# Closing a hand-written section ahead of the last store of a batched matrix product

One Trainium2 chip, one core. The metric is the device time of one execution in microseconds (us), lower is better. A store has *landed* when the last of the 16 DMA engines that share it has counted up its semaphore.

## The reference

```python
x: [16, 768, 512] f32      y: [16, 768, 1024] f32
out = np.einsum('bkm,bkn->bmn', x, y).astype(np.float32)      # [16, 512, 1024]
```

75.5 MB are read and 33.6 MB written. The kernel casts to bf16 on the chip, multiplies on TensorE and writes f32.

## The kernel before

The whole kernel body is one section of hand-written synchronisation (`tile_critical`) inside a Tile context. Tile is the layer that orders instructions and places semaphores by itself; in the section it leaves that to the author. SyncE issues all loads and stores; store `b` follows four steps behind its loads; VectorE casts, TensorE multiplies, ScalarE copies PSUM (the memory that TensorE writes its sums to) to one of five output buffers. At the end SyncE waits until every store has landed, then the section closes, then the context.

```python
    LAG = 4
    NO = 5
    ctx.enter_context(tc.tile_critical())          # closes when the function returns
    ...                                            # buffers, semaphores, loads' helper (cut)
    def store(b):
        if b < B - 2:
            nc.sync.wait_ge(groups, 2 * (b + 2))
        else:
            nc.sync.wait_ge(outs, b - (B - 3))
        nc.sync.dma_start(o_v[b], ob[b % NO][:]).then_inc(so[b % NO], 16)

    for b in range(B):
        ...                                        # loads of x and y (cut)
        if b >= LAG:
            store(b - LAG)
    for b in range(B - LAG, B):
        store(b)
    ...                                            # VectorE, GpSimd, TensorE (cut)
    for b in range(B):                             # ScalarE
        if b >= NO:
            nc.scalar.wait_ge(so[b % NO], 16 * (b // NO))
        for g in range(2):
            nc.scalar.wait_ge(groups, 2 * b + g + 1)
            cp = nc.scalar.copy(...)               # ob <- ps, half of the output of b
            if b < B - 1:
                cp.then_inc(room, 1)
        if b == B - 2:
            nc.scalar.drain().then_inc(outs, 1)
    cp.then_inc(outs, 1)

    for i in range(NO):
        nc.sync.wait_ge(so[i], 16 * len(range(i, B, NO)))
```

## Time and profile before

| of the kernel before | |
|---|---|
| timed | 262.55 us median of 3 (262.53 to 262.94) |
| the profiled execution | 261.94 us, span 260.2 us |
| last copy of ScalarE ends | 251.19 us |
| last store issued, landed | 251.22, 258.93 us |
| landing to end of span | 1.23 us |

The span runs from the first to the last instruction of the program in one profiled execution; times inside it count from its start.

### The profile page before, as it was taken

Reading aid. Unit: us, or ns where it says so; the run is one execution under the profiler, and the core shown is the slowest. Engines: PE = TensorE matmul, PEld = TensorE weight load, DVE = VectorE, ACT = ScalarE, POOL = GpSimd, SP = SyncE. Lnnn points to the kernel's source line nnn. Section 1 sums busy time; section 2 is a strip of 40 time slices with the busy share of each in tenths; the row PEclk is TensorE's granted clock in tenths of the full one; section 3 lists DMA queues with packets and bytes.
Section 4 is the critical chain, followed back from the end, with each engine's and each line's share of the span. In section 5 each row is a group of like instructions: output and inputs, shape, how many; then the busy total and the mean of one; then the engine's idle time right before and its main releaser. Section 6 shows DMA issues by size and latency. Waiting matters only on the chain. (4 is left out here: it accounts for less than half of the span.)

```text
span 260.2 us, 2506 instructions
## 1 busy us (share of the span) xinstructions
PE 188.3 (72%) x768; PEld 90.3 (35%) x768; DVE 82.0 (32%) x33; ACT 61.1 (23%) x33; POOL 0.2 (0%) x4
## 2 busy tenths in 40 slices
PE   0019999998938959499491995949869697785930
PEld 0004555554513525244250352514424243442410
DVE  0261644525241152511425214252232523125000
ACT  1000442243220222203222022220412204031220
POOL 0000000000000000000000000000000000000000
PEclk9999999999995979979999597997968989997985
DMA  7999989999999999999999999999999999999995
GB/s 272 418 476 408 476 378 469 393 368 461 438 398 469 388 479 423 411 441 393 458 431 441 433 388 464 408 436 446 396 456 418 464 416 423 451 385 431 438 403 227
DMA packets 4514, 109.07 MB, mean 419 GB/s; under 512 B 768, under 2 KB 768, under 8 KB 768
## 3 DMA queue, kind: packets, MB, share of 16 engines
q1 hardware_dynamic: 4512, 109.05, 98.3%
q14 instruction: 2, 0.02, 0.0%
HBM read 75.50 MB, written 33.55 MB: 419 GB/s over the span
## 5 line engine op out<-in xcount | busy, mean ns | idle before, releaser
L149 PE MATMUL ps<-yb,xb 128*128 x768 | 188.3, 411 | 61.0 <-PEq L144 61.0
L149 PEld LDWEIGHTS ps<-yb,xb 128*128 x768 | 90.3, 118 | 158.5 <-issue 92.6
L165 ACT COPY ob<-ps 128x2048 f32<-128x2048 f32 x32 | 59.8, 1869 | 184.8 <-PE ps L149 184.8
L127 DVE CAST yb<-ys 128x6144 bf16<-128x6144 f32 (+1 forms) x17 | 53.8, 3171 | 86.5 <-DMA ys<-in_y_dram 86.5
L123 DVE CAST xb<-xs 128x3072 bf16<-128x3072 f32 x16 | 28.2, 1760 | 69.7 <-DMA xs<-in_x_dram 65.2
L165 ACT ACT_TABLE_LOAD x1 | 1.3, 1283 | 5.3 <-issue 5.3
L189 POOL MEMSET const-bfloat16-1.0<- 128x1 bf16 x1 | 0.1, 102 | 0.0
L189 POOL MEMSET const-uint8-127<- 128x1 uint8 x1 | 0.1, 102 | 0.0
L189 POOL MEMSET const-float32-1.0<- 128x1 f32 x1 | 0.1, 99 | 0.0
L189 POOL MEMSET const-float32-0.0<- 128x1 f32 x1 | 0.1, 98 | 0.2 <-issue 0.2
## 6 DMA issues: line engine op xcount, KB each, us to landing
ys<-in_y_dram SPq DMA_DIRECT2D x16, 3072.0 KB, 28.2
out_dram<-ob SPq DMA_DIRECT2D x16, 2048.0 KB, 32.6
xs<-in_x_dram SPq DMA_DIRECT2D x16, 1536.0 KB, 29.8
```

The costliest lines, as they stand in the source:

```text
L123: nc.vector.tensor_copy(xb[:, i], xs[i][:]).then_inc(cast, 1)
L127: nc.vector.tensor_copy(yb[:, i, ks], ys[i][:, ks]).then_inc(cast, 1)
L149: mm = nc.tensor.matmul(ps[g][:, m, nt], x_w[:, bass.ds(s, 1), kt, mo], yb[:, bass.ds(s, 1), kt, nt * NF:(nt + 1) * NF], start=(kt == 0), ...
L165: cp = nc.scalar.copy(ob[b % NO][:, g * HB:(g + 1) * HB].rearrange("p m (t f) -> p m t f", f=NF), ps[g][:])
L189: nc = _bacc.Bacc("TRN2", target_bir_lowering=False, num_devices=1)
```

## The change

The intent is to take the closing of the section off the end of the kernel: the section closes while the queue is still busy with earlier stores; the last store is issued behind it by Tile, which also waits for it as it leaves the context. The hand-written waits shrink to stores 11, 12 and 13.

```diff
-    ctx.enter_context(tc.tile_critical())
+    section = ExitStack()
+    section.enter_context(tc.tile_critical())
...
-    for b in range(B - LAG, B):
+    for b in range(B - LAG, B - 1):
         store(b)
...
-    for i in range(NO):
-        nc.sync.wait_ge(so[i], 16 * len(range(i, B, NO)))
+    for b in range(B - LAG - 1, B - 2):
+        nc.sync.wait_ge(so[b % NO], 16 * (b // NO + 1))
+    section.close()
+
+    nc.sync.dma_start(o_v[B - 1], ob[(B - 1) % NO][:])
```

## The prediction

> **What bounds the kernel now.** I read the page of the kernel before first: the slices and the chain that ended last. Then I asked for four stretches of time around the last store, and last for SyncE's own waits and for every instruction of three source lines: the final waits (L174), the section's opening line, to which its closing code is also booked (L45), and the context's exit (L200).
>
> ```profile
> PE 188.3 (72%) x768; PEld 90.3 (35%) x768; DVE 82.0 (32%) x33; ACT 61.1 (23%) x33; POOL 0.2 (0%) x4
> ...
> DMA  7999989999999999999999999999999999999995
> ...
> PE 5%; ACT 1%; issue 0%
> ...
> out_dram<-ob SPq DMA_DIRECT2D x16, 2048.0 KB, 32.6
> ```
>
> The DMA row has 9 in nearly every slice, right up to the second last; no compute engine is above 72%. The chain explains only 6% of the span, because it starts at the last copy of ScalarE (end 251.2 us) and cannot go back through a DMA queue. So the bound is the transfers: 109 MB. A store takes a median of 32.6 us from issue to landing, because it queues behind loads and stores. From 41 to 251 us the queue moved 428 GB/s at a share of 1.00. Nothing in the change touches that body; whatever happens, happens after about 249 us.
>
> The end is read from two views. First the stretches (the last two columns are the share of the 16 DMA engines and GB/s; each stretch is 0.61 us, about one 16 KB packet on one engine, so share times 16 is the number of engines that began a packet in it):
>
> ```profile
> 251.40:252.01 0.61, 0.00 (x0) 0.00 (x0) 0.00 (x0) 0.00 (x0) 0.00 (x0) 0.63 0.44 188
> 252.01:252.62 0.61, 0.00 (x0) 0.00 (x0) 0.00 (x0) 0.00 (x0) 0.00 (x0) 0.50 1.01 430
> ...
> 256.20:256.81 0.61, 0.00 (x0) 0.00 (x0) 0.00 (x0) 0.00 (x0) 0.00 (x0) 0.50 1.01 430
> 256.80:257.41 0.61, 0.00 (x0) 0.00 (x0) 0.00 (x0) 0.00 (x0) 0.00 (x0) 0.50 0.26 108
> 257.41:258.02 0.61, 0.00 (x0) 0.00 (x0) 0.00 (x0) 0.00 (x0) 0.00 (x0) 0.50 0.19 81
> ```
>
> At 251.4 only 7 of 16 engines have work: the others are done with the second last store and starve until the last one, issued at 251.22, arrives at 252.05. After 256.8 only 4 engines, then 3, are moving data. These late ones never starved: their last packets start at 257.94 in the trace's packet records, and 8 packets of 0.611 us each make the store's share of an engine, so the latest began its share at 257.94 - 7 x 0.611 = 253.67, straight after its share of the store before. Those few set the landing at 258.93.
>
> Second, what SyncE does after that landing (SPq and the like are the sequencers; durations in ns, then first and last start in us):
>
> ```profile
> L45 SPq EVENT_SEMAPHORE  x3: 17/28/28, 259.1 to 259.3; - x3
> L45 SPq NOP  x2: 13/13/13, 0.7 to 259.4; - x2
> L45 SPq COMPARE_BRANCH  x1: 33/33/33, 258.9 to 258.9; - x1
> ...
> L174 SPq EVENT_SEMAPHORE  x2: 27/28/28, 251.6 to 254.1; - x2
> L200 SPq DRAIN  x3: 7/7/7, 259.4 to 259.8; - x3
> SPq L45 <- DMA out_dram<-ob: 4.8, 1, 4.8
> SPq L174 <- DMA out_dram<-ob: 2.5, 1, 2.5
> ```
>
> The five final waits have been folded into two semaphore instructions and into the section's closing branch: the branch at 258.944 carried the last of them (4.8 us of waiting). From there the section closes (one increment by SyncE, a DRAIN on each engine, two waits and a NOP on SyncE), which ends at 259.41. The context's exit follows, beginning with SyncE's DRAIN at 259.445 and ending with the span at 260.16. So there are two joins in a row after the last byte: 259.445 - 258.944 = 0.50 us for the section, 260.16 - 259.445 = 0.715 us for the context.
>
> **What the Trainium skill says.** "DMA: Bandwidth & Descriptors", Specifications, gives a fabric ceiling of 435 GB/s; the 428 GB/s of the long stretch agrees that the body is at the transfers' limit (and lies above the 358 GB/s that the same table gives as HBM's share of a core, so the measurement decides there). The same page, Queues, rings and completion order, says that each DMA engine consumes a queue's descriptors in ring order and that a semaphore increment lands only after that engine's earlier writes. The trace agrees: the stores' landings are 4.86, 4.87, 4.80 us apart at the end (244.40, 249.27, 254.13 and 258.93 for the last four). So the last store's full count of 16 also covers the second last store, for which the new code no longer waits. The same page, Latency and other measured facts, puts the first byte at about 600 ns; here it is 0.83 us from the issue, and I use that. "VectorE: DVE Perf Modes", The DRAIN you can't avoid, separates constant boilerplate DRAINs of about 12 ns from pipeline flushes; those at the end here are 7 to 64 ns, so what a join costs is the semaphore steps between engines.
>
> **The change, part by part.**
>
> (1) Removed: the five final waits. They take no time of their own; they end when the data land. Gain 0.
>
> (2) Added: three waits, for stores 11, 12 and 13. They landed at about 239.6, 244.4 and 249.27, all ahead of the end of ScalarE's last copy at 251.19. Cost 0, off the path.
>
> (3) Moved: the section's close, from after the landing to before the last issue. Its branch and SyncE's increment can now run at about 249.3, while ScalarE still copies. What is left after the copy: ScalarE's DRAIN and increment (before, the DRAIN of an earlier copy cost about 0.035 us more than the plain increment), one semaphore wait on SyncE and the NOP, 0.06 us each by their spacing at 259.27, 259.33, 259.40 and 259.445. That is 0.15 to 0.2 us, against 0.026 us from copy to issue now. So the last store is issued at about 251.35 to 251.45 in place of 251.22, 0.15 to 0.2 us later.
>
> (4) What the later issue costs. It moves the first packets of the starving engines from 252.05 to about 252.25. Those engines are done at 257.13, and the latest one at 258.56: they have 1.4 us to spare. The late engines need the descriptors by 253.67, 1.6 us after 252.05. Cost 0, as the delay is below 1.4 us.
>
> (5) The tail. The landing stays at 258.93; now the context's exit waits for it, at its first DRAIN or just ahead, and then takes its 0.715 us. The section's 0.50 us are gone from after the landing. Gain 0.50 us, less some 0.06 us if the exit gets a wait instruction of its own.
>
> Sum: span 260.2 - 0.5 = 259.7 us. The timed median lies 2.35 us above the profiled span (262.55 against 260.2) through what comes ahead of and after it; none of that changes. 262.55 - 0.45 = 262.1 us, 0.2% less.
>
> **Rivals.**
>
> A. The later issue reaches the end: the close costs more on SyncE than I think, and engines starve for it. Against it: 1.4 us to spare. If the close took all its 0.50 us after the copy, the landing would still not move. Only a delay over 1.4 us would eat into the gain, and one of 1.9 us would cancel it: 262.5.
>
> B. The last store is made to wait for the second last one too, through a dependence that Tile sees on the output or through a full join of queues. The issue would then be at about 254.3, and all engines would starve. From an issue to the first engines' count took 257.325 - 251.218 = 6.1 us, so the landing would be near 260.4, 1.5 us later than now, and the sum 262.55 + 1.5 - 0.5 = 263.5 us. For it: hand-written waits leave out exactly that store, and I have not seen what Tile makes of it. Against it: the section's raw semaphores are unknown to Tile, which can only wait for the section as a whole.
>
> C. The join is not removed but taken over: the exit now has waits of its own for a DMA and every engine, so that only 0.1 to 0.2 us go away: 262.4. The exit's DRAINs and semaphores (L200) exist before already and would only get one more wait, so I give this less weight.
>
> D. The body shifts by a changed instruction layout or another alignment of loads: no view shows a stall of that kind, and with DMA at 1.00 it would not show anyway.
>
> **Range and chances.** The mechanism makes 262.0 to 262.1; C and partial A 262.3 to 262.5; B 263.5. Three runs of before spread over 0.41 us, almost as much as the effect. I take 262.1, with 261.6 to 262.7 for 8 in 10. A 2% change would need 5.25 us, ten times the whole section's close, and nothing that follows the last landing is that long (1.23 us in all): faster 0.01, same 0.97, slower 0.02.
>
> **What would show it.** In the profile after: the last store issued at 251.3 to 251.5, counted from the span's start, with three stores waited for before 249.5; the section's DRAINs and semaphores (L45) between 249 and 251.5 and none after the landing; the last landing within 0.2 us of 258.9; from landing to the span's end 0.7 to 0.8 us in place of 1.23; the span near 259.7; 4 or 3 engines still at work at the end. I am wrong if the last store is issued after 252.5 (A) or after 254 (B), if more than 1 us follows the landing (C), or if the median moves by more than 0.7 us either way.

## The result, and the profile after

| | before | after |
|---|---|---|
| timed, first set | 262.54 us (4 runs, 262.36 to 262.94) | 262.27 us (4 runs, 261.99 to 262.47) |
| ratio of that set | | 0.9987, 95% interval 0.9970 to 1.0004 |
| profiled execution: last copy ends | 251.19 | 250.66 |
| last store issued | 251.22 | 250.88 |
| second last store landed | 254.13 | 255.09 |
| last store landed | 258.93 | 259.90 |
| landing to end of span | 1.23 | 0.79 |

A ratio is the mean time of one kernel's fast runs over that of the other's of the same rounds, so it is not quite the ratio of the medians quoted beside it. The change is within 2%, and slightly on the fast side. One set does not exclude zero; the experiments add two more.

The page of the changed kernel, the same rows as before:

```profile
span 260.7 us, 2506 instructions
...
PE 186.1 (71%) x768; PEld 89.8 (34%) x768; DVE 82.0 (31%) x33; ACT 61.1 (23%) x33; POOL 0.2 (0%) x4
...
DMA  7998999999899899989999989999998999999994
...
PE 9%; ACT 1%; issue 0%
```

The body is the same: DMA at 9 or close to it throughout, compute engines below 72%. Yet the profiled span is longer than before (260.7 against 260.2), although less happens after the landing. The profiled execution took 262.47 us, the slowest of its four; the one of before, 261.94, was faster than any of the four that were timed in that set. Two single executions cannot be subtracted here. They can be compared part by part.

First SyncE's instructions, by source line, in the changed kernel (durations ns min/median/max, then first and last start in us). L46 is the section, L175 the three waits, of which one has been folded into the section's branch, L181 the store that Tile issues, L207 the context's exit; the lines are picked from the views of these four and from that of the waits:

```profile
L175 SPq EVENT_SEMAPHORE  x1: 28/28/28, 250.2 to 250.2; - x1
L46 SPq COMPARE_BRANCH  x1: 33/33/33, 250.3 to 250.3; - x1
L46 SPq EVENT_SEMAPHORE  x3: 17/28/28, 250.5 to 250.7; - x3
L46 ACTq DRAIN  x1: 171/171/171, 250.5 to 250.5; - x1
L46 SPq NOP  x1: 13/13/13, 250.8 to 250.8; - x1
L181 SPq DMA_DIRECT2D out_dram<-ob x1: 332/332/332, 250.9 to 250.9; - x1
L207 SPq EVENT_SEMAPHORE  x3: 17/17/17, 259.9 to 260.6; - x3
L207 SPq DRAIN  x3: 7/7/7, 260.0 to 260.3; - x3
SPq L207 <- DMA out_dram<-ob: 8.7, 1, 8.7
```

The whole close, which before stood at 258.9 to 259.4 behind the landing, now stands at 250.3 to 250.8. ScalarE's DRAIN (171 ns here, 14 ns in e2, where the last copy was over before it) waits for the last copy, and the store follows 0.22 us after that copy instead of 0.03. The wait of 8.7 us for the last store has moved from the section's branch to the exit, where one wait (259.916 in the trace) stands ahead of the DRAIN (259.970): 0.05 us of new cost. From landing to end it is 0.79 us.

Then the DMA engines near the end of the changed kernel, as in the prediction (the last two columns are their share and GB/s):

```profile
251.40:252.01 0.61, 0.00 (x0) 0.00 (x0) 0.00 (x0) 0.00 (x0) 0.00 (x0) 0.68 1.02 430
...
256.20:256.81 0.61, 0.00 (x0) 0.00 (x0) 0.00 (x0) 0.00 (x0) 0.00 (x0) 0.50 0.32 134
256.80:257.41 0.61, 0.00 (x0) 0.00 (x0) 0.00 (x0) 0.00 (x0) 0.00 (x0) 0.50 0.25 107
257.41:258.02 0.61, 0.00 (x0) 0.00 (x0) 0.00 (x0) 0.00 (x0) 0.00 (x0) 0.50 0.13 54
258.02:258.63 0.61, 0.00 (x0) 0.00 (x0) 0.00 (x0) 0.00 (x0) 0.00 (x0) 0.50 0.06 27
258.63:259.24 0.61, 0.00 (x0) 0.00 (x0) 0.00 (x0) 0.00 (x0) 0.00 (x0) 0.50 0.06 27
```

All 16 engines begin a packet between 251.4 and 252.0, where 7 did before, because the copy happened to end earlier. Some ran dry here too, but sooner: by the packet records 8 of 16 had one in flight at 251.7, just when the first packets of the last store began. Most are done by 256.8; two go on (0.13 of 16), then a single one (0.06 of 16) to 259.5. So here the last landing is set by one engine that was late. The lateness was there before the change could act: store 13 had landed at 250.23, against 249.27 in the profile of before, and the section's branch comes only at 250.32. The second last store lands at 255.09, against 254.13, and the last one 4.81 us after that one here, 4.79 us there.

### The profile page after: what moved, and what is told of

It is laid out like the page before. It is cut to its first block, busy times and chain, and to the rows that moved or that the text cites. A ratio compares the mean times of both kernels' runs of the same rounds, so it can differ in the third digit from the quotient of the medians.

```text
span 260.7 us, 2506 instructions
## 1 busy us (share of the span) xinstructions
PE 186.1 (71%) x768; PEld 89.8 (34%) x768; DVE 82.0 (31%) x33; ACT 61.1 (23%) x33; POOL 0.2 (0%) x4
## 5 line engine op out<-in xcount | busy, mean ns | idle before, releaser
L150 PE MATMUL ps<-yb,xb 128*128 x768 | 186.1, 407 | 62.7 <-PEq L145 60.7
```

The source lines that it names most:

```text
L150: mm = nc.tensor.matmul(ps[g][:, m, nt], x_w[:, bass.ds(s, 1), kt, mo], yb[:, bass.ds(s, 1), kt, nt * NF:(nt + 1) * NF], start=(kt == 0), ...
```

## The experiments

My theory, in three parts: (a) closing the section costs about 0.5 us of SyncE's time wherever it stands, and behind the landing this is paid in full; (b) the later issue is free, because the latest DMA engines set the end and still have earlier work; (c) the landing's own scatter has nothing to do with the change. The main rivals: the landing comes later by as much as the tail got shorter; Tile's issue, not the early close, is what helps; the running dry of some engines matters.

**The changed kernel again, twice (e1, e9).** Edit: none.

> The changed kernel again, with more rounds, to size the gain. My theory (the section's 0.50 us leave the tail, 0.06 us of a new wait come in, the landing doesn't move): 0.4 to 0.5 us faster than before, ratio 0.9981 to 0.9985. Rival D0 (the landing moves later by about as much as the tail got shorter, as the one profile pair would have it: last landing 259.9 against 258.9): no gain, ratio 0.9995 to 1.001. In its profile both agree on 0.7 to 0.8 us from landing to the end.

> The changed kernel once more, to size the gain with the last set (two sets gave 0.9987 with intervals of 0.0016 either way). My theory: 0.44 us less after the landing (1.23 to 0.79 us in the profiles), the landing unchanged on average: ratio 0.9979 to 0.9989. Rival (the landing gives it back): 0.9995 or above.

Measured: e1 261.81 us (6 runs) against 262.51 (11 runs), ratio 0.9987 (0.9971 to 1.0003); e9 261.91 us (6) against 262.22 (11), ratio 0.9985 (0.9962 to 1.0007). With the first set these are three sets that agree; weighted by their intervals and taken as independent they give 0.9987, give or take 0.0010, so 0.35 us less (0.0013 x 262.5). That excludes no gain, if barely, and includes the 0.44 us of the tail; taken by itself no set does exclude it. The rival's range (0.9995 and above) is touched only at the upper end. e1 lies just outside the range expected of it, e9 inside. In all three profiles of the changed kernel 0.79 us follow the landing, and the last store lands 4.81, 4.84 and 4.82 us after the second last.

**One part alone: close early, issue by hand (e2, e10).**

```diff
-    for b in range(B - LAG, B - 1):
+    for b in range(B - LAG, B):
...
-    nc.sync.dma_start(o_v[B - 1], ob[(B - 1) % NO][:])
+    with tc.tile_critical():
+        nc.sync.wait_ge(so[(B - 1) % NO], 16 * ((B - 1) // NO + 1))
```

(With the wait written bare, in no section, the program did not build: its scheduling reported a deadlock. So it has no run.)

> One part alone: the last store is still issued by hand, inside the section (so 0.03 us after the copy, not 0.2), the five-engine section closes while it flies, and a second section holding only SyncE's wait for it stands behind. My theory: the close of five engines is off the tail, a close of one engine remains, 0.1 to 0.3 us; so 0.2 to 0.4 us faster than before, between before and the change. Rival (what helps is Tile's own issue of the store): no faster than before, ratio 0.9995 to 1.0005.

> The kernel with the second, SyncE-only section once more (0.9996 in the first set, its profile had 1.12 us after the landing against 1.23 before and 0.79 in the change): ratio 0.9990 to 1.0001, slower than the changed kernel of the same rounds by 0.2 to 0.4 us.

Measured: 262.29 us, 0.9996 (0.9983 to 1.0009), and 262.14 us, 0.9996 (0.9973 to 1.0019): 0.1 us, less than the 0.2 to 0.4 expected at first, and inside the range that the first expectation gave to its rival (0.9995 to 1.0005); e10 came out as expected, 0.3 us slower than the changed kernel of its rounds by the ratios (0.9996 - 0.9985). The times alone cannot tell why, the trace can. The lines of e2 after the landing, SyncE only, picked from two views (L208 is the exit, L181 the second section):

```profile
L208 SPq COMPARE_BRANCH  x1: 33/33/33, 259.4 to 259.4; - x1
L181 SPq EVENT_SEMAPHORE  x1: 17/17/17, 259.6 to 259.6; - x1
L181 SPq DRAIN  x1: 7/7/7, 259.7 to 259.7; - x1
L181 SPq NOP  x1: 13/13/13, 259.7 to 259.7; - x1
L208 SPq DRAIN  x3: 7/7/7, 259.8 to 260.1; - x3
```

A section of SyncE alone costs almost as much to close as one of five engines. From the branch at 259.413 to the exit's DRAIN at 259.775 it is 0.36 us, and a folded wait lies ahead of the branch; 1.14 us follow the landing, in both profiles (the 1.12 in the second expectation was a misreading), against 1.23 before and 0.79 in the change. The largest step is the branch itself, 0.155 us to the next instruction. So what is costly is SyncE's own series of branch, increment, DRAIN and NOP, and less the join of the other engines: of the 0.50 us before, two waits for other engines (0.06 and 0.07 us) are what drops out. My picture of a "join" was off here. It also says which half of the change matters: the wait for the last store must be in no section of its own, otherwise most of the cost is back behind the landing. In the change it is Tile's; issue and wait by Tile were not tried apart from each other, as the bare wait did not build.

**A later issue (e3, e11, e4).** In the changed kernel, ahead of the close, with n = 8 and n = 80:

```diff
+    nc.sync.wait_ge(outs, 2)
+    for _ in range(n):
+        nc.sync.sem_inc(idle, 1)
     section.close()
```

> The changed kernel with SyncE made to wait for ScalarE's last copy ahead of the close and then to do 8 semaphore steps of 0.067 us: the last store is issued about 1.0 us later than in the change (0.54 for the steps, 0.45 for the close, which now all lies after the copy). My theory (1.4 us to spare at least, because the latest DMA engines set the end): same time as the changed kernel within 0.15 us, and the same 0.7 to 0.8 us after the landing. Rival A (a later issue reaches the end): 1.0 us slower than the change.

> The changed kernel with the issue 0.7 to 1.0 us later once more (0.9992 in the first set): my theory says as the changed kernel of the same rounds within 0.2 us; the rival that a later issue reaches the end, 0.7 us or more slower than that.

> The same with 80 steps: issue 5.9 us later than in the change. My theory: 5.9 us less what there is to spare, 1.4 (profile of before) to 2.7 us (profile of after): 3.2 to 4.5 us slower than the change, about 265.4 to 266.8. Rival A (no slack): 5.9 us slower, 268.1. All 16 engines should begin and end the last store almost together.

Measured for n = 8: 262.02 us, 0.9992 (0.9979 to 1.0005), and 262.20 us, 1.0001 (0.9979 to 1.0022). The issue is 0.96 us after the copy in both profiles, 0.74 us later than in the change, and still the last store lands 4.82 us after the second last and 0.80 us remain. So these two executions lost nothing by it. The timed medians are 0.21 and 0.29 us above the change's of the same rounds, a little more than I allowed and well below the 0.7 to 1.0 of the rival. By the means of these runs e3 is 0.07 us slower and e11 0.44 us (95% intervals of 0.5 and 0.3 us either way), so the second is clear of zero. Part of that cannot come from the landing: the timed result exceeds the span by 1.92 us in the profiled executions of e2, e3, e10 and e11, and by 1.77 to 1.78 in the nine others, before and change among them; no view here shows why. Less this 0.14 us, e3 is 0.07 us faster and e11 0.30 us slower. So the full cost of the delay is excluded, a part of it is not: whether some executions with less lag pay for the delay stays open.

Measured for n = 80: 265.42 us, ratio 1.0124 (1.0097 to 1.0152), so 1.37% or 3.6 us above the change (1.0124 - 0.9987), while the issue came 5.5 us later (5.71 us after the copy against 0.22). About 1.9 us were absorbed, 0.7 us either way (its four runs lie between 264.42 and 266.29); in the profiled execution 2.7 us: the store landed at 262.22, which is 2.8 us later than 4.82 us after the second last (254.59). The stretches of that kernel show what absorbing means:

```profile
254.00:255.00 1.00, 0.00 (x0) 0.00 (x0) 0.00 (x0) 0.00 (x0) 0.00 (x0) 0.50 0.00 0
255.20:256.60 1.40, 0.00 (x0) 0.00 (x0) 0.00 (x0) 0.00 (x0) 0.00 (x0) 0.50 0.00 0
256.60:257.21 0.61, 0.00 (x0) 0.00 (x0) 0.00 (x0) 0.00 (x0) 0.00 (x0) 0.50 1.01 430
```

Once the queue has run empty, all 16 engines start together, and the 16 landings lie within 0.20 us of each other, in place of 1.5 to 2.9 us in the change. The lag of the late engines is what pays for a late issue. Both the time and the even start are as expected.

**Ten sections more behind the landing (e5).** Stores and waits in the section as before, then:

```diff
+    section.close()                               # the section's opening is as in the change (cut)
+    for _ in range(10):
+        with tc.tile_critical():
+            for e in (nc.tensor, nc.vector, nc.scalar, nc.gpsimd, nc.sync):
+                e.nop()
```

> All stores and waits in the section as before, and ten sections more behind it, each with one NOP on each of the five engines: ten joins more after the last landing. My theory (a section's join after the last landing is paid one to one in the timed median, 0.50 us for a close, something more for an opening): 5 to 7 us slower than before. Rival C (joins overlap or hide in what comes after the kernel): under 2 us.

Measured: 270.80 us against 262.39, ratio 1.0311 (1.0294 to 1.0329), so 8.2 us slower, above my 5 to 7. The trace says the same: 9.38 us follow the landing in place of 1.23, 8.15 more.

```profile
L182 SPq EVENT_SEMAPHORE  x30: 17/28/28, 260.9 to 268.4; - x30
L182 SPq NOP  x20: 13/13/18, 260.5 to 268.5; - x20
```

A section with nothing in it but a NOP on each engine (the trace has no record of these) takes 0.82 us on average. Nine of the ten steps from one to the next are 0.76 to 0.78 us, one is 1.19 and unexplained. The first took 0.77 (from its NOP at 260.521 to the next one's at 261.287), 0.25 of it for opening (to the branch at 260.770), the rest for the close and the step to the next. I had reckoned too little for the opening. What matters for (a): time behind the landing goes one to one into the timed result (8.2 for 8.15). So the 0.44 us of the change's tail are real time, too small for three sets of runs to size well.

**The wait for the second last store put back (e6).**

```diff
-    for b in range(B - LAG - 1, B - 2):
+    for b in range(B - LAG - 1, B - 1):
```

> The changed kernel with the hand-written wait for the second last store put back, so the section can close only when it has landed (rival B of the prediction made real). My theory: issue 0.6 us after that landing, then 6.1 to 6.9 us to the next landing in place of 4.8; so 1.5 to 2.5 us slower than the change. A theory in which the queue needn't be fed ahead of time: no slower than the change.

Measured: 264.26 us, ratio 1.0072 (1.0057 to 1.0088), so 1.9 us slower than before and 2.2 (1.0072 - 0.9987) than the change, as expected. The last store is issued at 255.02, 0.63 us after the landing it waited for, and lands at 261.34. This is the prediction's rival B made real; it costs more than the 1.0 us written there, which left the close out of the way to the issue (254.3 supposed, 255.0 found).

```profile
253.60:254.40 0.80, 0.00 (x0) 0.00 (x0) 0.00 (x0) 0.00 (x0) 0.00 (x0) 0.50 0.00 0
254.40:255.80 1.40, 0.00 (x0) 0.00 (x0) 0.00 (x0) 0.00 (x0) 0.00 (x0) 0.50 0.00 0
255.85:256.46 0.61, 0.00 (x0) 0.00 (x0) 0.00 (x0) 0.00 (x0) 0.00 (x0) 0.50 1.01 430
```

No packet starts for over 2 us, then all engines start one. The change is right to leave this store out of its waits.

**The last store in halves (e7 on the kernel before, e8 on the change).**

```diff
+        nc.sync.dma_start(o_v[b, :, :HB], ob[b % NO][:, :HB]).then_inc(so[b % NO], 16)   # b = 15: after its first copy
+        nc.sync.wait_ge(outs, 3)
+        nc.sync.dma_start(o_v[b, :, HB:], ob[b % NO][:, HB:]).then_inc(so[b % NO], 16)   # e7; in e8 without then_inc, by Tile, behind the close
+    ...                                            # ScalarE's count after the first copy; e7's last wait counts both halves (cut)
```

> The kernel before with its last store cut in two, the first half issued after the first of the two last copies (5 us earlier), so that no DMA engine runs dry at 251 to 252 us. My theory (the few latest engines set the end, and they never ran dry): same as before within 0.2 us. Rival (the starving of 9 of 16 engines for up to 0.8 us sets the end): 0.4 to 0.8 us faster.

> The two together: first half by hand in the section, the second half issued behind it by Tile. My theory: as the changed kernel within 0.2 us. Rival: 0.4 to 0.8 us faster than the changed kernel.

Measured: e7 262.60 us, ratio 1.0012 (0.9998 to 1.0026); e8 262.43 us, ratio 1.0000 (0.9986 to 1.0014). Neither is faster. In e7 the engines no longer run dry (a share of 0.98 at 251.4 where before had 0.44):

```profile
251.40:252.01 0.61, 0.00 (x0) 0.00 (x0) 0.00 (x0) 0.00 (x0) 0.00 (x0) 1.00 0.98 416
...
258.02:258.63 0.61, 0.00 (x0) 0.00 (x0) 0.00 (x0) 0.00 (x0) 0.00 (x0) 0.50 0.13 54
```

and still two engines are at work at 258.02, and the landing comes 4.84 us after the second last store's. So the running dry of the early engines did not set the end. e8 has the change's 0.79 us tail, but came out about 0.3 us above the change's ratio, more than the 0.2 us expected, and e7 0.3 us above before; the intervals overlap, and whether halves cost something by themselves is open. The two differ by 0.3 us in the same rounds (1.0012 - 1.0000), the change's gain once more, though not clear of noise.

No version beat the changed kernel beyond noise.

## Why the prediction was right

- **The bound, and where the change acts**: right. The body moves the same 428 to 429 GB/s from 41 to 251 us in both kernels.
- **(1), (2) waits removed and added cost nothing**: right, though closer than said. Store 13 landed at 250.23 in the profiled execution, 0.43 us ahead of the copy's end, not 2 us (the test "before 249.5" failed with it); SyncE's part of the close and the copy ended almost together. In e1 it was 1.9 us ahead.
- **(3) the issue is 0.15 to 0.2 us later**: 0.22, 0.19 and 0.22 us after the copy in three profiles, against 0.03. Right; the absolute 251.35 to 251.45 was not (250.88), as the copies end anywhere from 249.7 to 251.6 us.
- **(4) the later issue costs 0, with at least 1.4 us to spare**: supported for the most part. 0.74 us more left no mark in two traces, though a part of it may show in the times of e11; of 5.5 us more some 1.9 were absorbed on average. One reading under it was wrong: "at 251.4 only 7 of 16 engines have work" takes the packets begun in a stretch for the engines at work at its start. By the packet records 12 were at work at 251.4 and 7 at 252.0; the engines run dry one after the other. The sum rests on the last packets and is not touched.
- **(5) 0.50 us leave the tail, 0.06 come back**: 1.23 to 0.79 us, so 0.44. Right to the step: 0.05 us for the new wait.
- **The landing stays at 258.93, within 0.2 us**: this test failed as I wrote it (259.90). In eleven profiles of kernels that issue within 1 us of the copy or in halves, changed or not, the last landing lies between 258.93 and 259.98, always 4.79 to 4.85 us after the second last store's, which itself lies between 254.13 and 255.13. The scatter is that of the late engines, there already before the change acts: the second last landing lies between 254.13 and 255.13 in three profiles with the body of before (before, e5, e7) and between 254.17 and 255.09 in the other eight. The span of 259.7 failed with it: 260.7, 260.1 and 260.1 in three profiles.
- **The 2.35 us between timed median and span**: mis-sized, as I set a span against the median of other, slower executions. Of one execution it is 1.78 us in both profiles (262.47 - 260.69, 261.94 - 260.16). As only a difference was taken, no harm came of it.
- **The sum, 0.45 us less**: 0.27 us by the medians of the first set, 0.35 us by the ratios of three. The median predicted was 262.1; 262.27, 261.81 and 261.91 were found. That the medians fit proves little: the range of 261.6 to 262.7 also holds the median of before, 262.54, so no gain at all would have passed. The mechanism rests on the 0.44 us of the tail, the same in three profiles, and on e5.

Rival A is refuted as a full cost of small delays, B did not happen (and costs 1.9 us when made to), C is refuted by the 0.79 us. For D, a body moved by the change, there is no sign in the landings above.

## What to carry to other kernels

Work behind the last landing is paid one to one, so look in the profile at what SyncE does after it, instruction by instruction, and move what does not depend on the data ahead of the last issue, as long as the queue still has earlier work to cover the delay. Do not wait for that earlier work, or the cover is gone. Size such a change by the part of the trace it touches and not by subtracting two spans: here single executions of one kernel scatter by up to 1.7 us (261.22 to 262.94 for before), the gain is 0.4.

## What the Trainium skill lacked or had wrong

- "DMA: Bandwidth & Descriptors", Latency and other measured facts, gives about 600 ns to the first byte and does not say from where it counts. Here the first packet began 0.83 us after the start of the issuing instruction, which is 0.50 us after its end, with all engines idle as well (e6: 255.02 to 255.36 for the instruction, 255.86 for the packet).
- The same page names two DMA engines as usually slower, but not that lag builds up. The spread of one transfer's 16 landings grew from 1.1 us (at 15 us) to 2.6 us in the profile of before, and from 1.2 to 3.5 in that of after, in jumps (after: 1.5 at 60 us, 2.2 at 76, 2.9 at 93, 3.3 at 125), and was not made up for good while the queue was full; once the queue had run empty (e4, e6) it was 0.2. In the packet records the slow packets are those of loads (48 KB: 1.84 us as a rule, up to 1.0 us more), not of stores (0.61 to 0.65), and many come in groups, near 56, 120 and 152 us in both of these profiles. The cause is open.
- No page gives the cost of ending a hand-written section: 0.50 us for five engines, about 0.4 for SyncE alone, and 0.82 us on average for an empty one opened and closed.
